# Two-part fp16 tables and states for the S5 scan of the first mixer, with the scan's inputs moved ahead in VectorE's order

## The chip, the cores and the metric

The kernel runs on one core of a Trainium2 chip. The metric is the device time of one execution in microseconds (us), as the median of several runs; less is better. The engines are named as in the profile: PE is TensorE's matrix products and PEld its weight loads, DVE is VectorE, ACT is ScalarE, POOL is GpSimd, and SP is SyncE, which here issues most of the transfers.

## The reference

The whole program is two residual networks one behind the other, at D = 1024 and T = 512 positions. Only the first mixer of the first one is touched. Its heart is S5: 32 groups of 16 channels, each with 64 complex states that decay and turn from position to position.

```
def _even_mixer(h, ...):
    proj = h @ w_in                       # 1024 -> 2048
    u_pool, u_ssm, z = proj[:512], proj[512:1024], proj[1024:]
    y_pool = _multiscale_pool(u_pool, pool_w, pool_scale)
    y_ssm = _s5(u_ssm, ...)
    return (concat(y_pool, y_ssm) * silu(z)) @ w_out

def _s5(u, log_dt, a, b, c, d_skip, w_glu):     # a, b, c complex
    abar = exp(a * dt); bb = (abar - 1) / a * b
    x[t] = abar * x[t-1] + bb @ u[t]            # 32 groups, 64 states
    y = real(c @ x) + d_skip * u
    val, gate = split(y @ w_glu)
    return val * sigmoid(gate)
```

## The kernel before, in words

**The projections.** Every large product is made in fp16 with both operands cut into a high and a low half: `form1` (L329 to 339) runs, for each of eight blocks of 128 rows, high by high (L336), low input by high weights (L337) and high input by low weights (L338), 24 products of 128x512 into one PSUM bank. `wload` and `wsplit` fetch a block of weights through SP's queue, write the high half on ACT (L283, with the factor `WS`) and the low half on DVE (L284). `split` (L290 to 292) does the same for activations, with the low half on POOL or on a given engine.

**The mixer.** `even` (L799 on) makes 16 projections of `ev_in` (384 products), then eight of `glu` (96) and eight of `ev_out` (192): 672 products in all. The first four are the scan's inputs: for each, DVE multiplies the PSUM bank by the norm's factor into `uS` (L821) and a DMA writes it to a buffer `ud` in device memory, from which it is read back in another layout. `s5_params` (L588 on) makes powers of the decay (`pr`, `pi`, by products at L563 to 568), the factors `k`, and the tables `bb` and `bd`.

**The scan** goes in four quarters q of eight groups each, in fp32. `s5_phases`, for each second quarter, makes tables of cosine and sine (`tr`, `ti`) by doubling, on DVE and POOL in turns, with the scratch tiles `ph`. `s5_tables` makes the output tables `CR` and `CI` on DVE with POOL's products `cw` (L702 to 708), the response of eight positions by products into `aq` (L714), which goes by `kt` and a buffer `kd` into eight shifted copies in `Tm` (SP's queue, L724), and the input tables: `bs` on DVE with `cw` on POOL (L733 to 735), turned on PE (L739) and copied by ACT to `bt` (L740). `s5_scan` loads `Ug`, runs 16 products of `bt` (L761), turns the result by four DVE products `sz` (L766 to 769), scans on DVE (L775, L776), turns back to the states `Sr` (DVE) and `Si` (POOL), and runs eight groups of three products into two banks: `Tm` by `Ug` (L787), `CR` by `Sr` (L788), `CI` by `Si` (L789). ACT copies them to `yg` (L791), which goes to device memory and back as `ys`.

**Behind the scan** in the code stand the four pool groups: a projection to the tile `up` (one buffer), running sums on POOL in `usa` and `usb` (one buffer each, L843), the difference `pd` on DVE (L846 to 848), another projection `zsp` and one fp32 product with `pool_w` (L854). Then come four gates `zs`, the `glu` products, which need `ys`, and `ev_out`.

**What sets the order.** The kernel is written on a tile scheduler, which puts each engine's instructions into one list, by the order of the code, a model of times, and the tiles that are free; on the chip each engine goes through its list in order. Projections take one of three PSUM banks `mm`; the first pool product and the norm use two banks `a`; the tables and the scan take turns on three banks `aq` by `aux()`. `mm()` looks at a list `self.first` first: its entries name the bank group of the next projections, before the standard `mm` holds. Ahead of the change the list is empty.

## Time and profile before

| | |
|---|---|
| median of 3 runs | 2562.06 us (2561.75 to 2565.82) |
| the profiled execution | 2564.81 us, span 2563.0 us |
| mean granted TensorE clock | 0.977 |
| PE busy | 2470.0 us (96%), 14547 instructions |
| PEld busy | 1255.7 us (49%) |
| DVE busy | 1363.2 us (53%) |
| ACT busy | 974.0 us (38%) |
| POOL busy | 738.9 us (29%) |
| DMA | 240.32 MB, 94 GB/s on average |

The span is the time from the first to the last instruction on the core; the execution's own time holds what lies around it, too. A matrix product's end is modelled and products are pipelined, so that one line of order of time says "0.38 us" for products that follow each other at 0.22. The granted clock is a share of TensorE's full speed. The first mixer fills the first 10% of the span.

### The profile page before, as it was taken

The numbers are of one execution on the slowest core, as the hardware profiler recorded it, in microseconds if no ns is written. First come the engines' busy times: TensorE is split into PE (matmuls) and PEld (weight loads), VectorE is DVE, ScalarE is ACT, GpSimd is POOL, SyncE is SP. The second block draws the span as 40 slices with busy tenths as digits, with TensorE's granted clock in tenths as the row PEclk, the third lists the DMA queues.
The fourth block names the chain that finished last, engine by engine and source line by source line (L and its number), as shares of the span: only waits on it lengthen the run. The fifth ranks groups of instructions, "written<-read, shape, count | busy, mean of one in ns | idle before, by whom it ended". The sixth has DMA issues, their size and how long they took to land.

```text
span 2563.0 us, 37095 instructions
## 1 busy us (share of the span) xinstructions
PE 2470.0 (96%) x14547; PEld 1255.7 (49%) x14547; DVE 1363.2 (53%) x2297; ACT 974.0 (38%) x1686; POOL 738.9 (29%) x634
## 2 busy tenths in 40 slices
PE   7998989999999999999999999999999999999998
PEld 3554434444444456674444444444457565444445
DVE  8846891753333577765433334333345777733334
ACT  4223666443322434333423223323223566523322
POOL 5611850333320244332333201333003121333300
PEclk9899989999999999999999999999999999999999
DMA  4223211233333432113333333333335101233333
GB/s 161 84 74 99 91 50 42 76 98 107 99 105 117 133 87 68 40 46 122 107 107 99 101 100 104 99 104 100 97 108 166 64 25 46 95 99 107 97 104 124
DMA packets 112440, 240.32 MB, mean 94 GB/s; under 512 B 39688, under 2 KB 51848, under 8 KB 112264
## 3 DMA queue, kind: packets, MB, share of 16 engines
q1 hardware_dynamic: 97760, 230.08, 29.3%
q10 hardware_dynamic: 14504, 7.87, 1.1%
q8 instruction: 114, 1.87, 0.3%
q14 instruction: 62, 0.51, 0.1%
HBM read 222.95 MB, written 7.34 MB: 90 GB/s over the span
## 4 chain that ended last, share of the span: by engine, by line
PE 83%; DVE 6%; issue 4%; POOL 3%; DMA 2%; ACT 2%; SPq 0%; ACTq 0%; POOLq 0%; DVEq 0%
PE b L337 17%; PE b L336 17%; PE b L338 17%; PE b L540 6%; PE b L541 6%; PE b L539 6%; POOL cv L966 2%; PE b L1205 1%; PE b L1626 1%; DVE wl L284 1%; PE mm L337 1%; PE mm L338 1%; PE mm L336 1%; PE b L1646 1%; PE b L1562 1%
## 5 line engine op out<-in xcount | busy, mean ns | idle before, releaser
L283 ACT ACTIVATE wh<-st 128x1024 f16<-128x1024 f32 (+6 forms) x432 | 422.7, 981 | 1069.0 <-PE b L337 666.9
L336 PE MATMUL b<-hh,wh 128*128 128x512 f16 x2096 | 799.0, 383 | 22.7 <-ACT hh L291 7.9
L337 PE MATMUL b<-hl,wh 128*128 128x512 f16 x2096 | 801.8, 383 | 1.2 <-POOL hl L292 1.0
L338 PE MATMUL b<-hh,wl 128*128 128x512 f16 x2096 | 799.8, 383 | 0.4 <-DVE wl L284 0.4
L284 DVE SCALAR_TENSOR_TENSOR wl<-st,wh 128x1024 f16<-128x1024 f32 (+6 forms) x432 | 507.3, 1176 | 367.5 <-ACT wh L283 365.9
L337 PEld LDWEIGHTS <-wh 128*128 128x128 f16 x2320 | 229.8, 99 | 300.8 <-issue 43.1
L336 PEld LDWEIGHTS <-wh 128*128 128x128 f16 x2320 | 230.2, 99 | 288.8 <-issue 24.3
L338 PEld LDWEIGHTS <-wl 128*128 128x128 f16 x2320 | 229.5, 99 | 284.8 <-issue 23.1
L539 PE MATMUL b<-fh,wh 128*128 128x512 f16 x660 | 250.1, 379 | 0.0
L540 PE MATMUL b<-fl,wh 128*128 128x512 f16 x660 | 250.1, 379 | 0.0
L541 PE MATMUL b<-fh,wl 128*128 128x512 f16 x660 | 250.1, 379 | 0.0
L528 POOL TENSOR_TENSOR sg<-sg,rho 128x512 f32<-128x512 f32 x88 | 153.6, 1747 | 292.6 <-ACT sg L527 282.0
L292 POOL TENSOR_TENSOR fl<-f,fh 128x512 f16<-128x512 f32 x88 | 139.9, 1590 | 265.6 <-ACT fh L291 265.4
L531 DVE SCALAR_TENSOR_TENSOR f<-b,sg 128x512 f32<-128x512 f32 x88 | 60.8, 691 | 246.0 <-PE b L338 239.9
L362 DVE TENSOR_TENSOR sg<-b,rho 128x512 f32<-128x512 f32 x88 | 60.4, 691 | 232.2 <-PE b L338 228.8
L292 POOL TENSOR_TENSOR hl<-nh,hh 128x512 f16<-128x512 f32 x42 | 54.6, 1307 | 288.3 <-ACT hh L291 288.3
L336 PE MATMUL mm<-hh,wh 128*128 128x512 f16 x224 | 88.3, 396 | 15.7 <-ACT hh L431 6.9
L539 PEld LDWEIGHTS <-wh 128*128 128x128 f16 x660 | 64.6, 98 | 78.0
L540 PEld LDWEIGHTS <-wh 128*128 128x128 f16 x660 | 64.6, 98 | 77.9
L541 PEld LDWEIGHTS <-wl 128*128 128x128 f16 x660 | 64.6, 98 | 77.8
L966 POOL TENSOR_TENSOR cv<-cv,cvt 128x512 f32<-128x512 f32 x60 | 88.0, 1469 | 14.5 <-ACT cvt L965 10.2
L337 PE MATMUL mm<-hl,wh 128*128 128x512 f16 x224 | 88.5, 397 | 3.0 <-DVE hl L432 2.2
(616 smaller groups left out, 3044.4 us busy)
## 6 DMA issues: line engine op xcount, KB each, us to landing
st<-in_gu_a SPq DMA_DIRECT2D x88, 512.0 KB, 3.5
st<-in_gu_b SPq DMA_DIRECT2D x88, 512.0 KB, 3.5
st<-in_dn_b SPq DMA_DIRECT2D x36, 512.0 KB, 3.5
st<-in_dn_a SPq DMA_DIRECT2D x32, 512.0 KB, 3.5
st<-in_od_in SPq DMA_DIRECT2D x24, 512.0 KB, 3.5
st<-in_ab_in SPq DMA_DIRECT2D x22, 512.0 KB, 3.5
st<-in_cd_in SPq DMA_DIRECT2D x16, 512.0 KB, 3.6
st<-in_ev_in SPq DMA_DIRECT2D x15, 512.0 KB, 3.7
```

The lines of the kernel that those rows point to most:

```text
L283: nc.scalar.activation(wh[:, s], st[:, s], AF.Copy, scale=WS)
L284: nc.vector.scalar_tensor_tensor(wl[:, s], st[:, s], WS, wh[:, s], op0=ALU.mult, op1=ALU.subtract)
L292: (eng or self.nc.gpsimd).tensor_sub(lo, src, hi)
L336: self.nc.tensor.matmul(ps, wh[:, s], xh[:, k], start=(k == 0), stop=False)
L337: self.nc.tensor.matmul(ps, wh[:, s], xl[:, k], start=False, stop=False)
L338: self.nc.tensor.matmul(ps, wl[:, s], xh[:, k], start=False, stop=(k == kn - 1))
L528: nc.gpsimd.tensor_mul(sg, sg, self.rho)
L531: nc.vector.scalar_tensor_tensor(f, ps, 1.0 / FS, sg, op0=ALU.mult, op1=ALU.mult)
L539: nc.tensor.matmul(ps, wh[:, s], fh[:, k], start=(k == 0), stop=False)
L540: nc.tensor.matmul(ps, wh[:, s], fl[:, k], start=False, stop=False)
L541: nc.tensor.matmul(ps, wl[:, s], fh[:, k], start=False, stop=(k == KF - 1))
L966: G.tensor_add(cv, cv, t)
```

## The change

Five numbers of the scan are put into fp16 halves, so that its products are made like the projections, in three passes (high by high, low by high, high by low) into the same banks.

- The inputs: behind each `uS`, ACT writes a high half and DVE a low half (`uh`, in the pool groups' tile `usa`), and `ud` and `Ug` hold two parts.
- `Tm`: the high half of `kt` on ACT, the low one on DVE, two parts of 128x1024 in fp16. Its 64 DMAs are shared: the high parts on SP's queue, the low ones on ACT's.
- The output tables: `s5c` is multiplied by `WS` once; `CR` and `CI` become scratch tiles (in the place of `bs0` and `bs1`), and a tile `C` takes their halves, the high ones by ACT, the low ones by POOL.
- `bt`: the high half on ACT with the factor `WS`, the low half on DVE straight from PSUM.
- The states: `Sp`, high by ACT, low by DVE.
- The factor's inverse `IWS` is taken in DVE's four products `sz` and in ACT's copies `yg`.

Two lines concern the order: `after()` gives the scheduler an edge without a semaphore, by which the first `CR` stands behind the last `uS` on DVE; and the first five projections take the banks `mm`, `mm`, `mm`, `aq`, `aq`.

```diff
+    def after(self, n, p):
+        self.tc.add_manual_dep(n.ins, p.ins.name, mybir.DependencyInfo(
+            mybir.DependencyClass.NoSync, mybir.DependencyReason.DATA), reason="in this order")
...
         nc.scalar.dma_start(S["c"], A["s5_c"])
+        nc.scalar.activation(S["c"], S["c"], AF.Copy, scale=WS)
...
-        CR = R["CR"] = qp.tile([P, 4, 9, 16], F32, name="CR")
-        CI = R["CI"] = qp.tile([P, 4, 9, 16], F32, name="CI")
+        CR = tp.tile([P, 4, 9, 16], F32, name="CR", tag="bs0")
+        CI = tp.tile([P, 4, 9, 16], F32, name="CI", tag="bs1")
...
-        V.tensor_tensor(CR, pw(pr), cb(0), op=ALU.mult)
+        n = V.tensor_tensor(CR, pw(pr), cb(0), op=ALU.mult)
+        if q == 0:
+            self.after(n, S["u"])
...
-        kt = tp.tile([P, P], F32, name="kt")
-        nc.scalar.activation(kt, ps, AF.Copy)
-        kd = self.dr.tile([P, P], F32, name=f"kd{q}")
+        kt = tp.tile([P, 2, P], F16, name="kt")
+        self.split(kt[:, 0], kt[:, 1], ps, V)
+        kd = self.dr.tile([P, 2, P], F16, name=f"kd{q}")
         nc.sync.dma_start(kd, kt)
-        Tm = R["T"] = qp.tile([P, 8, P], F32, name="Tm")
+        Tm = R["T"] = qp.tile([P, 2, 8, P], F16, name="Tm")
...
         for s in range(8):
-            nc.sync.dma_start(Tm[s * 16:(s + 1) * 16, :, (7 - s) * 16:P], kv[:, :, 0:(s + 1) * 16])
+            for e in range(2):
+                (nc.scalar if e else nc.sync).dma_start(
+                    Tm[s * 16:(s + 1) * 16, e, :, (7 - s) * 16:P], kv[:, e, :, 0:(s + 1) * 16])
+        C = R["C"] = qp.tile([P, 2, 2, 4, 8, 16], F16, name="C")
+        for r, t in enumerate((CR, CI)):
+            self.split(C[:, 0, r], C[:, 1, r], t[:, :, 1:9])
...
-            bt = qp.tile([P, 4, P], F32, name=f"bt{part}")
+            bt = qp.tile([P, 2, 4, P], F16, name=f"bt{part}")
...
-            nc.scalar.activation(bt, ps.rearrange("p (a b) -> p a b", a=4), AF.Copy)
+            nc.scalar.activation(bt[:, 0], ps, AF.Copy, scale=WS)
+            V.scalar_tensor_tensor(bt[:, 1], ps, WS, bt[:, 0], op0=ALU.mult, op1=ALU.subtract)
...
+        three = ((0, 0), (0, 1), (1, 0))
...
-                    nc.tensor.matmul(ps[hs, part, g], R["B"][part][:, g, hs], Ug[:, 2 * g + h], start=True, stop=True)
+                    for a, b in three:
+                        nc.tensor.matmul(ps[hs, part, g], R["B"][part][:, a, g, hs], Ug[:, b, 2 * g + h],
+                                         start=(a + b == 0), stop=(a == 1))
...
-        V.tensor_tensor(u[0], xr, ct, op=ALU.mult)
...
+        for o, x, y in zip(u, (xr, xi, xi, xr), (ct, st, ct, st)):
+            V.scalar_tensor_tensor(o, x, IWS, y, op0=ALU.mult, op1=ALU.mult)
...
+        Sp = qp.tile([P, 2, 2, 4, 64], F16, name="Sp", bufs=1)
+        for r, t in enumerate((Sr, Si)):
+            self.split(Sp[:, 0, r], Sp[:, 1, r], t, V)
...
-            nc.tensor.matmul(ps[:, g // 2], R["T"][:, g], Ug[:, g], start=True, stop=False)
-            nc.tensor.matmul(ps[:, g // 2], cr, Sr[h, g // 2], start=False, stop=False)
-            nc.tensor.matmul(ps[:, g // 2], ci, Si[h, g // 2], start=False, stop=True)
+            for a, b in three:
+                nc.tensor.matmul(ps[:, g // 2], R["T"][:, a, g], Ug[:, b, g], start=(a + b == 0), stop=False)
+            for r in range(2):
+                for a, b in three:
+                    c = R["C"][h, a, r, g // 2].rearrange("p j h -> p (j h)")
+                    nc.tensor.matmul(ps[:, g // 2], c, Sp[h, b, r, g // 2], start=False, stop=(r + a == 2))
...
+            self.first = ["mm", "mm", "mm", "aq", "aq"]
             uS = sp.tile([P, 4, 8, 64], F32, name="uS")
-            ud = self.dr.tile([4, 8, 16, 8, 64], F32, name="ud")
+            ud = self.dr.tile([4, 2, 8, 16, 8, 64], F16, name="ud")
...
-                V.tensor_mul(uS[:, m].rearrange("p s c -> p c s"), cs(ps), cs(self.rho))
-                nc.sync.dma_start(ud[m].rearrange("g h s c -> (g h) s c"), uS[:, m])
+                S["u"] = V.tensor_mul(uS[:, m].rearrange("p s c -> p c s"), cs(ps), cs(self.rho))
+                up = ek.tile([P, 2, 8, 64], F16, name="uh", tag="usa", bufs=1)
+                self.split(up[:, 0], up[:, 1], uS[:, m], V)
+                nc.sync.dma_start(ud[m].rearrange("e g h s c -> (g h) e s c"), up)
```

The lines of the changed kernel stand 5 or 6 further down in the first part and 13 to 23 further in the scan: the projection's products are L341 to 343, `uS` is L842, the input products L778, the output products of the states L809.

**On DVE, around the scan's inputs.** Before, the first three `uS` stand behind four table products, `CR` and `CI` (the names with `k` are small factors of the tables, `wl` a low half of weights):

```order
L655 TENSOR_TENSOR k_314<-k_314,k_315 128x16
L284 SCALAR_TENSOR_TENSOR wl<-st,wh 128x1024
L702 TENSOR_TENSOR CR<-pr,s5c 128x576 x2
L705 TENSOR_TENSOR CI<-pi,s5c 128x576 x2
L656 TENSOR_TENSOR ki<-k_314,den 128x16
L821 TENSOR_TENSOR uS<-mm,rho 128x64x8 x3
L704 TENSOR_TENSOR CR<-CR,cw_547 128x576
L708 SCALAR_TENSOR_TENSOR CI<-CI,cw_548 128x576
```

In the change the first two stand among the small products that make the powers (`pr`, `pw_0`), and the first low half `uh` follows:

```order
L656 TENSOR_TENSOR k_316<-pi,s5a 128x16
L644 TENSOR_TENSOR m_301<-m_301 128x16
L842 TENSOR_TENSOR uS<-mm,rho 128x64x8 x2
L636 TENSOR_TENSOR pr<-mag,cs 128x16
L645 TENSOR_TENSOR m_301<-m_301 128x16
L297 TENSOR_TENSOR uh<-uS,uh 128x512
L568 TENSOR_TENSOR pw_0_271<-pr 128x16
```

The inputs have moved ahead of the powers, and so of all tables.

**On PE, behind the outputs of the first scan.** Before, the last of its output products and the turning of a later `bs` are followed by projection products (`hh`, `wh`, `wl` are their halves):

```order
L787 MATMUL aq<-Ug,Tm 128x64
L788 MATMUL aq<-Sr,CR 128x64
L789 MATMUL aq<-Si,CI 128x64
L739 MATMUL aq<-ident,bs_730 128x128 x4
L338 LDWEIGHTS wl
L338 MATMUL mm<-hh,wl 128x512
L336 LDWEIGHTS wh
L336 MATMUL mm<-hh,wh 128x512
```

In the change the next scan's input products follow:

```order
L809 LDWEIGHTS C
L809 MATMUL aq<-Sp,C 128x64
L752 MATMUL aq<-ident,bs_871 128x128 x4
L778 LDWEIGHTS bt_863
L778 MATMUL aq<-Ug,bt_863 64x64
```

No projection product stands at this place any more.

**On PE, behind the outputs of the last scan.** Before, 314 projection products follow, the first of them in the midst of a group of 24:

```order
L787 MATMUL aq<-Ug,Tm 128x64
L788 MATMUL aq<-Sr,CR 128x64
L789 MATMUL aq<-Si,CI 128x64
L337 LDWEIGHTS wh
L337 MATMUL mm<-hl,wh 128x512
L338 LDWEIGHTS wl
L338 MATMUL mm<-hh,wl 128x512
```

In the change a pool product comes first, and then 432 projection products, with three more pool products among them:

```order
L809 LDWEIGHTS C
L809 MATMUL aq<-Sp,C 128x64
L877 MATMUL a<-pd,pool_w 128x512
L341 LDWEIGHTS wh
L341 MATMUL mm<-hh,wh 128x512
L342 LDWEIGHTS wh
L342 MATMUL mm<-hl,wh 128x512
```

So 118 projection products and all four pool products have moved behind the last scan.

## Rows read from the trace of the kernel before

**Rows 1.** Busy time by stretch: from:to, us, busy (instructions), PEclk, DMA share, GB/s.

```profile
24.00:72.00 48.00, 36.70 (x210) 17.86 (x209) 47.12 (x125) 13.71 (x19) 38.86 (x48) 0.83 0.32 99
110.00:120.00 10.00, 10.00 (x33) 7.05 (x33) 4.12 (x6) 1.59 (x4) 2.46 (x2) 0.51 0.42 122
165.00:238.00 73.00, 69.93 (x316) 31.00 (x315) 39.40 (x52) 28.49 (x46) 1.15 (x13) 0.98 0.38 117
```

**Rows 2.** PE in order of time: start us, us, instruction, [idle before <-releaser].

```profile
37.92 0.58 PE L336 MATMUL mm<-hh,wh 128*128 128x512 f16 x1 [6.44 <-DVE uS L821]
...
165.16 0.61 PE L337 MATMUL mm<-hl,wh 128*128 128x512 f16 x1
...
168.12 0.39 PE L338 MATMUL mm<-hh,wl 128*128 128x512 f16 x1
...
172.02 0.38 PE L338 MATMUL mm<-hh,wl 128*128 128x512 f16 x1
...
237.89 0.38 PE L338 MATMUL mm<-hh,wl 128*128 128x512 f16 x1
```

**Rows 3.** DVE in order of time, up to the first scan.

```profile
28.41 0.18 DVE L631 TENSOR_TENSOR pi<-mag,sn 128x16 f32<-128x16 f32 x1
...
31.80 0.18 DVE L655 TENSOR_TENSOR k<-k,k 128x16 f32<-128x16 f32 x1
...
36.85 2.79 DVE L821 TENSOR_TENSOR uS<-mm,rho 128x512 f32<-128x512 f32 x3
...
66.31 0.41 DVE L766 TENSOR_TENSOR sz<-aq,tr 128x252 f32<-128x252 f32 x1
```

**Rows 4.** PE in order of time, a pool product.

```profile
88.13 1.02 PE L854 MATMUL a<-pd,pool_w 128*128 128x512 f32 x2
```

**Rows 5.** DVE in order of time, subtractions and additions of the input tables.

```profile
88.54 0.68 DVE L735 TENSOR_TENSOR bs<-bs,cw 128x512 f32<-128x512 f32 x1
...
120.07 3.15 DVE L735 TENSOR_TENSOR bs<-bs,cw 128x512 f32<-128x512 f32 x2 [0.33 <-POOL cw L734]
```

**Rows 6.** Groups by line, DVE, 0 to 205 us: count | busy, mean ns | idle before.

```profile
L284 DVE SCALAR_TENSOR_TENSOR wl<-st,wh 128x1024 f16<-128x1024 f32 x18 | 24.0, 1341 | 2.6 <-ACT wh L283 2.6
```

**Rows 7.** POOL in order of time, its first large table product.

```profile
31.85 5.04 POOL L706 TENSOR_TENSOR cw<-pr,s5c 128x576 f32<-128x576 f32 x1 [1.10 <-DVE pr L567]
```

**Rows 8.** Groups by line, POOL, 24 to 160 us, shapes apart.

```profile
L734 POOL TENSOR_TENSOR cw<-pi,bb 128x512 f32<-128x512 f32 x8 | 10.9, 1368 | 5.1 <-DVE CR L704 4.4 <-DVE CI L708 0.7
L706 POOL TENSOR_TENSOR cw<-pr,s5c 128x576 f32<-128x576 f32 x4 | 9.1, 2280 | 1.1 <-DVE pr L567 1.1
...
L703 POOL TENSOR_TENSOR cw<-pi,s5c 128x576 f32<-128x576 f32 x4 | 5.9, 1483 | 0.0
L292 POOL TENSOR_TENSOR hl<-zsp,hh 128x512 f16<-128x512 f32 x4 | 5.5, 1364 | 11.8 <-ACT hh L291 11.8
```

**Rows 9.** Tile ph alone, by stretch: us, DVE and POOL busy, PEclk, DMA.

```profile
24.00:160.00 136.00, 21.61 (x42) 22.03 (x42) 0.87 0.29 86
```

**Rows 10.** The last scan in order of time, on DVE and POOL.

```profile
148.13 0.41 DVE L766 TENSOR_TENSOR sz<-aq,tr 128x252 f32<-128x252 f32 x1
...
154.00 0.80 POOL L568 TENSOR_TENSOR Si<-sz,sz 128x256 f32<-128x256 f32 x1
```

**Rows 11.** Groups by line, ACT, 0 to 205 us: copies out of PSUM.

```profile
L740 ACT ACTIVATE bt<-aq 128x512 f32<-128x512 f32 x8 | 4.7, 595 | 4.2 <-PE aq L739 4.2
L791 ACT ACTIVATE yg<-aq 128x256 f32<-128x256 f32 x4 | 1.5, 385 | 26.4 <-PE aq L789 26.4
```

**Rows 12.** PE in order of time, output products of the first scan.

```profile
78.46 0.43 PE L787 MATMUL aq<-Ug,Tm 128*128 128x64 f32 x2
...
79.41 0.43 PE L787 MATMUL aq<-Ug,Tm 128*128 128x64 f32 x2
```

**Rows 13.** PE in order of time, fp16 products of 64 columns in a later stage.

```profile
2008.88 0.29 PE L1656 MATMUL b<-nv,nat 128*128 128x64 f16 x4
```

**Rows 14.** Tile Tm, 0 to 200 us: durations ns min/median/max, first and last start.

```profile
L724 SPq DMA_DIRECT2D Tm<-kd x32: 318/428/752, 56.8 to 134.9; - x32
```

More of the change, by code (lines that the diff above doesn't have):

```diff
@@ L715, in s5_tables @@
             nc.tensor.matmul(o, S["bd"][:, 1, gg], CI[:, g, 0:8].rearrange("p j h -> p (j h)"), start=False, stop=True)
-        kt = tp.tile([P, P], F32, name="kt")
-        nc.scalar.activation(kt, ps, AF.Copy)
-        kd = self.dr.tile([P, P], F32, name=f"kd{q}")
+        kt = tp.tile([P, 2, P], F16, name="kt")
+        self.split(kt[:, 0], kt[:, 1], ps, V)
+        kd = self.dr.tile([P, 2, P], F16, name=f"kd{q}")
         nc.sync.dma_start(kd, kt)
-        Tm = R["T"] = qp.tile([P, 8, P], F32, name="Tm")
-        G.memset(Tm, 0.0)
-        kv = kd.rearrange("(g h) x -> h g x", h=16)
+        Tm = R["T"] = qp.tile([P, 2, 8, P], F16, name="Tm")
+        G.memset(Tm.bitcast(F32), 0.0)
+        kv = kd.rearrange("(g h) e x -> h e g x", h=16)
         for s in range(8):
-            nc.sync.dma_start(Tm[s * 16:(s + 1) * 16, :, (7 - s) * 16:P], kv[:, :, 0:(s + 1) * 16])
+            for e in range(2):
[4 more added lines that the diff above has]
+            self.split(C[:, 0, r], C[:, 1, r], t[:, :, 1:9])
         sh = [P, 4, 8, 16]
@@ L739, in s5_tables @@
                 nc.tensor.transpose(ps[:, i * P:(i + 1) * P], bs[:, i].rearrange("p s h -> p (s h)"), self.ident)
-            nc.scalar.activation(bt, ps.rearrange("p (a b) -> p a b", a=4), AF.Copy)
+            ps = ps.rearrange("p (a b) -> p a b", a=4)
+            nc.scalar.activation(bt[:, 0], ps, AF.Copy, scale=WS)
+            V.scalar_tensor_tensor(bt[:, 1], ps, WS, bt[:, 0], op0=ALU.mult, op1=ALU.subtract)
             R["B"].append(bt)
@@ L746, in s5_scan @@
         V, G = nc.vector, nc.gpsimd
-        Ug = qp.tile([P, 8, 64], F32, name="Ug")
-        uv = ud[q].rearrange("g h s c -> h s g c")
+        Ug = qp.tile([P, 2, 8, 64], F16, name="Ug")
+        uv = ud[q].rearrange("e g h s c -> h s e g c")
         for s in range(8):
             nc.sync.dma_start(Ug[s * 16:(s + 1) * 16], uv[:, 7 - s])
+        three = ((0, 0), (0, 1), (1, 0))
         br = qp.tile([P, 4, 64], F32, name="br")
@@ L765, in s5_scan @@
         u = [i[:, :, 0:63] for i in t]
-        V.tensor_tensor(u[0], xr, ct, op=ALU.mult)
-        V.tensor_tensor(u[1], xi, st, op=ALU.mult)
-        V.tensor_tensor(u[2], xi, ct, op=ALU.mult)
-        V.tensor_tensor(u[3], xr, st, op=ALU.mult)
+        for o, x, y in zip(u, (xr, xi, xi, xr), (ct, st, ct, st)):
+            V.scalar_tensor_tensor(o, x, IWS, y, op0=ALU.mult, op1=ALU.mult)
         V.tensor_add(br[:, :, 1:64], u[0], u[1])
@@ L784, in s5_scan @@
             h = slice((g % 2) * 64, (g % 2) * 64 + 64)
-            cr = R["CR"][h, g // 2, 1:9].rearrange("p j h -> p (j h)")
-            ci = R["CI"][h, g // 2, 1:9].rearrange("p j h -> p (j h)")
-            nc.tensor.matmul(ps[:, g // 2], R["T"][:, g], Ug[:, g], start=True, stop=False)
-            nc.tensor.matmul(ps[:, g // 2], cr, Sr[h, g // 2], start=False, stop=False)
-            nc.tensor.matmul(ps[:, g // 2], ci, Si[h, g // 2], start=False, stop=True)
+            for a, b in three:
[4 more added lines that the diff above has]
+                    nc.tensor.matmul(ps[:, g // 2], c, Sp[h, b, r, g // 2], start=False, stop=(r + a == 2))
         yg = ek.tile([P, 8, 64], F32, name="yg", bufs=1)
-        nc.scalar.activation(yg[:, 0::2], pe[:, 0:4], AF.Copy)
-        nc.scalar.activation(yg[:, 1::2], po[:, 0:4], AF.Copy)
+        nc.scalar.activation(yg[:, 0::2], pe[:, 0:4], AF.Copy, scale=IWS)
+        nc.scalar.activation(yg[:, 1::2], po[:, 0:4], AF.Copy, scale=IWS)
         nc.sync.dma_start(yd[q].rearrange("t h g c -> (t h) g c"), yg)
```

## The prediction

> **What bounds the kernel now.** I read the stretches of the first mixer first, then TensorE's and VectorE's order of time in them, then the costs of their instructions. TensorE (PE) is busy in 96% of the whole span, so what counts is when it gets through its list. The mixer's last projection product starts at 237.89 us, the last scan's outputs are finished at 165.16, and between them stand 314 products of 128x512 with little idle time [rows 1, 2]. Ahead of that PE is not full: it is busy for 36.70 of the 48 us from 24 to 72 [rows 1], 6.44 of them lost at 37.92 to the scan inputs uS, which VectorE (DVE) makes only at 36.85 [rows 2, 3]. DVE itself is busy for 47.12 of those 48 us and GpSimd (POOL) for 38.86 [rows 1]. So at first the tables are made by a full DVE and POOL while PE fills the time with projection products; after 165 us PE alone decides.
>
> **What the order changes.** It decides more than the number formats. Now 248 projection products (672 in the mixer, less 110 ahead of the first table products and 314 behind the last scan) lie between the products of the four scans and hide the scans' waits. In the new order 158 stand ahead of the first table products, 82 more up to the last scan's outputs, and 432 behind these, with the four pool products (L854) among them. Once scan 0 has begun, PE holds a single projection (24 products) up to the last scan's outputs. The cause is in the bank list: the fifth call of mm() takes an aq bank, which is given out after the 24 of the scans, and with it the first pool group, its single tile up and all that follows wait for scan 3. The comparison is therefore one of ends: when must the last scan's outputs be finished for 432 products to end where 314 end now?
>
> **Break-even.** A projection product takes 0.2167 us (18 of them from 168.12 to 172.02, [rows 2]); 432 take 93.6. Four pool products take 1.02 each [rows 4], 4.1. The first seven run slowly, as from 165.16 to 168.12 now: 2.96 us in place of 1.52, 1.4 more [rows 2]. Idle time stays: 165 to 238 holds 3.07 us of it now [rows 1]; the wait for the scan's output ys is part of that and will be covered by 88 products, so I take 2. Sum 101.1; the end now is 237.89 + 0.22 = 238.1. Hence the last scan must be through at **137.0 us**; each microsecond later is one lost, each earlier one gained. The stages after the mixer keep their work; the scheduler moved some rows in them, which I set at 0, with 3 either way for the range.
>
> **Up to the first scan.** Today the uS instructions stand behind four table products on DVE; now two of them stand just behind the instruction that starts at 28.41 [rows 3], so they begin at about 28.5 instead of 36.85 and PE's 6.44 us go. Then DVE has three uS (2.79), two low halves uh (0.68 each, as any such instruction of 512 elements, [rows 5]), a weight split (1.3, [rows 6]) and the small instructions that take it from 28.41 to 31.80 now [rows 3], some 8.4 us with their overlaps: 36.9. There POOL begins its tables, which is where it gets to work now too, its first being held up to 36.89 [rows 7]. So the early inputs free PE but not POOL. Up to what scan 0 needs, POOL has four cw of 128x576 (5.7: two L703, and two L706 without the one of 5.04 us), four cw of 128x512 (5.5), three new low halves of C (4.1, by the subtraction of the same shape) [rows 7, 8], and both phase tables: 22.0 us with the bb products [rows 9], of which the last two instructions, 0.8 each, are not needed. 35.7 us, so 72.6. A table step and a weight split on DVE and the hand-overs between the engines add 3.4 (at least 1, at most 7). Scan 0's first DVE instruction: **76 us**, against 66.31 now [rows 3].
>
> **A round, from one scan's first DVE instruction to the next one's.** (1) From there to the state Si DVE and POOL take 6.7 us in the last scan, a ys among it (148.13 to 154.80, [rows 10]). (2) Ahead of the state on DVE stand the next quarter's four bs: 0.68 each, 2.7; where POOL works two take 3.15, so 4.5 or more at worst [rows 5]. (3) The halves of the states are new: ACT's high and DVE's low half, 0.4 each (the yg copies are of 256 elements too, [rows 11]): 0.8. (4) 72 products in fp16. Now eight groups of three fp32 products take 0.95 us each [rows 12]; fp16 products of 64 columns with new weights follow each other at 0.03 us (four end 0.29 after the first starts, each being 0.19, [rows 13]): 2.2 for a scan. That is a real saving of 5.4 us of PE per scan, but it now lies in a chain in which PE waits. [...] I take the half rate: 4.3. (5) Two yg and two bt high halves on ACT [rows 11], one low half on DVE: 0.8 + 1.2 + 0.7 = 2.7. (6) Half of the Tm transfers are now issued from ACT's queue, and wait there for kd; three stand between yg and bt at 0.43 each [rows 14]: between 0 and 1.3, I take 0.6. (7) The second 24 of the scan's 48 input products: 0.7, or 1.4 at the half rate. Sum 6.7 + 2.7 + 0.8 + 4.3 + 2.7 + 0.6 + 1.4 = **19.2** (15.8 to 21.7). CR and CI of the next quarter lie in DVE's gap while PE and ACT are at work, and cost nothing as long as (4) to (7) last longer than their 2.7. The doubled Tm pieces and the Ug loads have a round's time and lie beside the chain. The scale factors ride in instructions that exist; the one on s5c is a short ACT instruction long before its use.
>
> **Sum.** 76 + 3 x 19.2 + 11.8 (the last round's 1, 3 and 4) = 145.4, that is 8.4 later than 137.0. The profiled execution took 2564.8, so 2573.2; it lies 2.7 above the median of the runs, 2562.1, so **2570.5**. With the lower bounds of the round it is 76 + 47.4 + 9.7 = 133.1 (4 faster), with the upper ones and 80 for the first scan 156.9 (20 slower). A measurement of this kernel tells some 0.2% from no change, 5.1 us.
>
> **Rivals.** (a) *PE keeps its full rate* in the short bursts: the round is 16.4, the last scan through at 134.9, the time 2560.0, no change to be told. Against it the 0.51 [rows 1]; for it, that fp16 passes are shorter and denser. (b) **Faster:** the chain hides behind DVE's own work, since POOL loses ten pool additions in this stretch and weight splits fall away. Then a round is what DVE itself has to do: 6.0 up to Sr, bs 2.7, CR and CI 2.7, bt 1.4, Sp 0.8, kt 0.3, 13.9 us [rows 5, 10]; 76 + 41.7 + 9.7 = 127.4, 9.6 faster, 2552.5. It decides where the round falls below 17. For it: nothing else stands in PE's queue, where scans are now held up by projections. (c) *DVE and POOL exclude each other.* A bs that takes 0.68 took 1.6 in the pair at 120.07 beside POOL [rows 5]. If each such instruction waits out the other engine's, a round is POOL's 11.7 (two cw of each kind and two C halves 8.3, four of the scan's 3.4 by Si's 0.80 and more, [rows 8, 10]) plus DVE's 9 on two SBUF inputs and 1.9 others, 22.6: 76 + 67.8 + 11.8 = 155.6, 2580.7. [...] (d) *ys holds DVE up.* It stands in DVE's queue ahead of the states; a wait for its transfer may return each round. I keep that within the upper bound.
>
> **Chances.** Forecast 0.45, (a) 0.22, (b) 0.18, (c) 0.15. Slower by over 0.2%: 0.35 of the forecast and all of (c), 0.50. Within it: the rest of the forecast, 0.10, of (a) 0.17, of (b) 0.01, together 0.28. Faster: 0.17 of (b) and 0.05 of (a), 0.22. The range runs from (b) to (c), 2552 to 2582; on the slower side alone it would be 2567 to 2582.
>
> **What would show it.** After: uS from about 28.5 and no wait of PE for it; scan 0 at 74 to 80; DVE idle for several microseconds a round, waiting for ACT's bt and yg; rounds of 18 to 21 us; a granted clock near 0.5 from 80 to 145; 432 products without gaps behind the last scan. Wrong if rounds are near 14 to 16, if PE holds its full rate there, or if the last outputs come ahead of 137 us.

## The result, and the profile after

The changed kernel takes **2592.99 us** (median; 2591.52 to 2601.98), the one before 2562.24 beside it: ratio 1.0124, 95% interval [1.0099, 1.0149], 31 us slower. The forecast was slower, but by 8.4 us, with 20 as the end of the range.

The profiled execution is the slowest of the four, 2601.98 us with a span of 2600.2, 37.2 above the one of before. Of these, 26.7 lie in the first mixer, whose last product moved from 237.89 [rows 2] to 264.57. Of the rest, 2.9 and 6.5 lie in two later stages (867 to 1232 and 1918 to 2224 us in the kernel before). All 17 kernels profiled here do the same work there, but the scheduler put it into another order in many of them, and these two stages took 358 to 372 and 303 to 312 us, without regard to which mixer was faster. Four other stages, whose order is the same in all 17, took 346.7, 343.3, 342.8 and 318.3 us in every one. In the second of the two the change's order took 311.2 to 312.0 in three kernels, the order of before 305.4 and 306.3 in two. So an edit can cost some 6 us in a stage that it does not touch, by the order there.

The change's own execution is late besides: its first `uS` starts at 31.77, and at 29.4 to 30.3 in the other fp16 versions. Without these 1.8 us (e3 and e5, with the same order up to there, start at 29.9), an estimate gives the mixer some 25 of the median's 31 and the later stages some 6.

The kernel before alone ran between 2557.85 and 2571.39 in 22 runs. So the mixer's end is compared in what follows beside the time, and of the times no difference under some 4 us is read.

Busy time by stretch in the kernel after, columns as in [rows 1]:

```profile
24.00:72.00 48.00, 42.78 (x206) 19.07 (x204) 44.24 (x127) 18.25 (x26) 29.21 (x50) 0.94 0.43 125
80.00:140.00 60.00, 24.34 (x315) 17.51 (x316) 45.45 (x68) 9.11 (x21) 31.86 (x34) 0.50 0.25 58
110.00:120.00 10.00, 3.44 (x38) 2.50 (x38) 9.26 (x12) 0.83 (x2) 5.75 (x8) 0.50 0.13 21
```

Up to 72 us PE has gained, as forecast (42.78 busy in place of 36.70). From 80 to 140 it is busy for 24.34 of 60 us, at a granted clock of 0.50. VectorE (DVE) in order of time, from the inputs to the last scan:

```profile
31.77 1.94 DVE L842 TENSOR_TENSOR uS<-mm,rho 128x512 f32<-128x512 f32 x2
...
70.80 0.86 DVE L708 TENSOR_TENSOR CR<-pr,s5c 128x576 f32<-128x576 f32 x1
71.59 0.87 DVE L713 TENSOR_TENSOR CI<-pi,s5c 128x576 f32<-128x576 f32 x1
...
77.37 1.27 DVE L755 SCALAR_TENSOR_TENSOR bt<-aq,bt 128x512 f16<-128x512 f32 x2
...
79.99 2.17 DVE L284 SCALAR_TENSOR_TENSOR wl<-st,wh 128x1024 f16<-128x1024 f32 x1
82.08 0.41 DVE L785 SCALAR_TENSOR_TENSOR sz<-aq,tr 128x252 f32<-128x252 f32 x1
...
90.20 1.43 DVE L568 TENSOR_TENSOR sz<-zr,tr 128x256 f32<-128x256 f32 x1
91.56 1.44 DVE L570 TENSOR_TENSOR sz<-zr,ti 128x256 f32<-128x256 f32 x1
...
105.27 0.42 DVE L785 SCALAR_TENSOR_TENSOR sz<-aq,tr 128x252 f32<-128x252 f32 x1 [0.28 <-PE aq L778]
...
115.05 1.43 DVE L297 TENSOR_TENSOR Sp<-Si,Sp 128x256 f16<-128x256 f32 x1
116.40 1.43 DVE L297 TENSOR_TENSOR Sp<-Sr,Sp 128x256 f16<-128x256 f32 x1
...
127.91 0.42 DVE L785 SCALAR_TENSOR_TENSOR sz<-aq,tr 128x252 f32<-128x252 f32 x1 [1.40 <-PE aq L778]
...
132.28 0.75 DVE L892 SCALAR_TENSOR_TENSOR ys<-uS,ev_vec,ys 128x512 f32<-128x512 f32 x1 [2.65 <-DMA Ug<-ud]
...
139.11 0.41 DVE L297 TENSOR_TENSOR Sp<-Si,Sp 128x256 f16<-128x256 f32 x1
...
149.31 0.42 DVE L785 SCALAR_TENSOR_TENSOR sz<-aq,tr 128x252 f32<-128x252 f32 x1 [1.40 <-PE aq L778]
...
153.73 0.75 DVE L892 SCALAR_TENSOR_TENSOR ys<-uS,ev_vec,ys 128x512 f32<-128x512 f32 x1 [2.69 <-DMA ys<-yd]
```

The scans begin at 82.08, 105.27, 127.91 and 149.31, so the rounds are 23.2, 22.6 and 21.4. PE in order of time: the output products of scan 1, the last of scan 3, the mixer's end.

```profile
117.89 0.48 PE L809 MATMUL aq<-Sp,C 64*128 64x64 f16 x10 [2.13 <-DVE Sp L297]
...
122.11 0.50 PE L809 MATMUL aq<-Sp,C 64*128 64x64 f16 x6
...
162.10 0.50 PE L809 MATMUL aq<-Sp,C 64*128 64x64 f16 x6
...
264.57 0.38 PE L343 MATMUL mm<-hh,wl 128*128 128x512 f16 x1
```

The last scan is through at 162.6, in place of the 145.4 forecast and the 137.0 needed; behind it lie 102.0 us to the last product's start at 264.57, where the sum had 100.9 (101.1 to its end). So the comparison of ends held, and the 17.2 us by which the forecast missed the last output lie ahead of 162.6.

### The profile page after: what moved, and what is told of

Same layout as the page of the kernel before. It is cut to its first block, busy times and chain, and to the rows that moved or that the text cites. A ratio compares the mean times of both kernels' runs of the same rounds, so it can differ in the third digit from the quotient of the medians.

```text
span 2600.2 us, 37533 instructions
## 1 busy us (share of the span) xinstructions
PE 2467.7 (95%) x14707; PEld 1252.3 (48%) x14707; DVE 1377.3 (53%) x2321; ACT 982.8 (38%) x1707; POOL 742.3 (29%) x642
## 4 chain that ended last, share of the span: by engine, by line
PE 81%; DVE 6%; issue 4%; POOL 3%; ACT 2%; DMA 2%; SPq 1%; POOLq 0%; DVEq 0%; ACTq 0%
PE b L341 16%; PE b L342 16%; PE b L343 16%; PE b L546 5%; PE b L545 5%; PE b L544 5%; POOL cv L989 2%; PE b L1228 1%; PE b L1649 1%; PE mm L342 1%; PE mm L341 1%; PE mm L343 1%; DVE wl L284 1%; PE b L1669 1%; PE b L1585 1%
## 5 line engine op out<-in xcount | busy, mean ns | idle before, releaser
L341 PE MATMUL b<-hh,wh 128*128 128x512 f16 x2096 | 797.3, 382 | 26.7 <-ACT hh L296 9.4
L341 PEld LDWEIGHTS <-wh 128*128 128x128 f16 x2320 | 229.8, 99 | 292.7 <-issue 24.4
L989 POOL TENSOR_TENSOR cv<-cv,cvt 128x512 f32<-128x512 f32 x60 | 88.5, 1478 | 14.5 <-ACT cvt L988 10.2
L341 PE MATMUL mm<-hh,wh 128*128 128x512 f16 x208 | 81.2, 394 | 10.9 <-ACT hh L436 8.1
L342 PE MATMUL mm<-hl,wh 128*128 128x512 f16 x208 | 81.3, 393 | 3.3 <-DVE hl L437 3.2
```

The costliest lines, as they stand in the source:

```text
L341: self.nc.tensor.matmul(ps, wh[:, s], xh[:, k], start=(k == 0), stop=False)
L342: self.nc.tensor.matmul(ps, wh[:, s], xl[:, k], start=False, stop=False)
L989: G.tensor_add(cv, cv, t)
```

## The experiments

Each kernel was timed beside the kernel before (medians of 2562.96 to 2564.61). Times in us; all but the median are from one profiled execution of each kernel. `sz` is a scan's first DVE product, so a round runs from one scan's first `sz` to the next one's. The gap is the idle time of PE behind the last output, up to the mixer's last product:

| | first sz | rounds, last part | last output | mixer's last product | gap | median |
|---|---|---|---|---|---|---|
| before | 66.3 | 28.4, 28.6, 24.8, 17.1 | 165.2 | 237.9 | 3.1 | 2562.2 |
| the change | 82.1 | 23.2, 22.6, 21.4, 13.3 | 162.6 | 264.6 | 2.2 | 2593.0 |
| e1 list of 4 | 83.3 | 37.4, 24.6, 18.9, 14.2 | 178.5 | 246.5 | 9.1 | 2571.7 |
| e2 fp32, list of 5 | 68.3 | 26.7, 22.3, 21.6, 17.2 | 156.1 | 256.2 | 1.9 | 2583.7 |
| e3 ys late | 80.3 | 23.2, 22.0, 18.7, 12.7 | 156.8 | 258.2 | 2.6 | 2585.5 |
| e4 Tm on SP | 80.0 | 22.2, 28.3, 17.4, 15.5 | 163.4 | 270.3 | 5.7 | 2602.7 |
| e5 bt early | 76.1 | 23.5, 23.5, 20.3, 13.1 | 156.5 | 257.6 | 2.5 | 2590.1 |
| e6 no cw | 77.1 | 21.4, 20.0, 20.7, 13.7 | 152.8 | 253.9 | 1.9 | 2579.0 |
| e15 low halves on ACT | 74.1 | 20.6, 19.9, 18.5, 11.8 | 144.9 | 246.7 | 3.0 | 2575.3 |

**What takes the cover away: the bank list or the format?** The cover is the projection products that keep PE busy while the scans wait. Two kernels part the two causes. The first is the change with

```diff
-            self.first = ["mm", "mm", "mm", "aq", "aq"]
+            self.first = ["mm", "mm", "mm", "aq"]
```

> The changed kernel with the bank list shortened by its fifth entry, so that the first pool group's projection takes a standard bank again; all fp16 parts stay. PE then has projection products and pool products among the scans' products, and 261 projection products in place of 432 behind the last scan's outputs. Theory (the order, through the bank list, took the cover from PE): PE is busy nearly throughout from 80 to 160 us, its granted clock there is over 0.8, the rounds may take 20 to 27 us, the last outputs come at 160 to 175 us, and 261 products take 57 behind them: the mixer ends at 219 to 235 against 238 before, so 2540 to 2562 us, 30 to 50 below the change. Rival (the splits, their queueing and the sharing of DVE and POOL cost it, whatever PE has to do meanwhile): within 8 of the change, 2583 to 2603.

It took 2571.71, ratio to before 1.0036 [1.0025, 1.0048]: 21 us less than the change, from one entry of a list. 261 products now stand behind the last scan. Its stretch from 80 to 140 us:

```profile
80.00:140.00 60.00, 52.01 (x396) 25.41 (x394) 53.40 (x79) 17.06 (x32) 43.35 (x51) 0.94 0.28 75
```

PE is busy for 52.01 in place of 24.34, at 0.94. The theory holds for the cover; the time lies 10 above its range, since the last outputs came at 178.5 and not by 175, and PE then waited (below). The second is the kernel before, all in fp32, with the list of five and nothing else:

> The kernel before with the list of five banks alone, everything in fp32. PE has 432 projection products behind the last scan and one group of 24 among the scans, as in the change. Theory (the list is the cause): slower than before by 20 to 45, 2582 to 2607 us, with a granted clock near 0.5 among the scans. Rival (the fp16 parts are the cause): within 8 of before, 2554 to 2570.

It took 2583.73, 1.0079 [1.0061, 1.0098], 20 slower than before, and PE's row from 80 to 140 us shows a granted clock of 0.50 again (34 projection products still lie among its scans, where 24 were expected):

```profile
80.00:140.00 60.00, 48.57 (x283) 40.04 (x282) 31.07 (x46) 6.44 (x14) 20.19 (x24) 0.50 0.21 57
```

So the list costs some 20 us in either format (18.1 and 18.3 at the mixer's end), and the fp16 parts with the cover another 8 to 9; the rival that the format alone is the cause falls.

The change without its edge of `after()` was not run. But the early inputs need neither the edge nor the list nor the halves `uh`: e8 below has the states' products in fp16 and nothing else, and its DVE begins the inputs as early, ahead of the first large table product:

```profile
29.37 1.93 DVE L829 TENSOR_TENSOR uS<-mm,rho 128x512 f32<-128x512 f32 x2
...
36.26 1.75 DVE L706 TENSOR_TENSOR CI<-pi,s5c 128x576 f32<-128x576 f32 x1
```

With the list alone, in e2, they start at 37.96, behind four table products as before. So the output tables' new form brings the inputs forward; which part of it does so (the scaled `s5c`, or `CR` and `CI` as scratch tiles) is not shown.

**What makes the exposed rounds long?** Five kernels with the list of five, as in the change. First, the early ys instructions behind the last scan's states:

```diff
-                V.scalar_tensor_tensor(v, uS[:, m]..., vec[:, 1, m:m + 1], v, ...)
+                n = V.scalar_tensor_tensor(v, uS[:, m]..., vec[:, 1, m:m + 1], v, ...)
+                self.after(n, self.last)      # the last low half of Sp
```

> The changed kernel with the three early ys instructions placed behind the last scan's states on DVE. In the change's trace DVE waits 2.65 and 2.69 us for ys in two rounds, with 0.75 for the instruction itself, ahead of the scan instruction zr. Theory (these waits lie in the chain): 5 to 7 us less than the change, 2586 to 2588. Rival (zr waits just as long for POOL's bi or another transfer): within 2 of the change, 2591 to 2595.

2585.50, 7.5 less. The third round fell from 21.4 to 18.7, the last part from 13.3 to 12.7, the others by 0.6 at most, 3.9 in all. The waits for ys lie in the chain: `zr` stands right behind them. The mixer ends 6.3 earlier, but 1.8 of that lie ahead of the first scan, where this kernel is the changed one: so much differs between executions. In the later stages e3 has nearly the order of the kernel before, and part of the 7.5 lies there.

The transfers of `Tm` all on SP:

```diff
-                (nc.scalar if e else nc.sync).dma_start(
+                nc.sync.dma_start(
```

> The changed kernel with all 64 Tm transfers issued from SP. In the change's trace three of them stand on ACT between yg and bt in two rounds and take 1.27 with 0.94 of idle time behind. Theory (they lengthen the round): 3 to 6 us less, 2587 to 2590. Rival (SP's queue then holds up the transfers of yg, ys and kd behind the Tm ones): no gain, or slower by up to 6, 2592 to 2599.

2602.65, 10 more: the rival holds, though the loss is above its range. The second round became 28.3 long, and PE's order of time names the transfer that came too late there:

```profile
128.95 1.50 PE L778 MATMUL aq<-Ug,bt 128*64 128x64 f16 x48 [8.36 <-DMA Ug<-ud]
```

The scan's inputs `Ug` stand in SP's queue, from 126.17 on, behind transfers of `Tm` (from 111.48) and ys (from 122.03). In the last part PE waited another 5.76 for `Tm` itself. The first scan came 2.1 earlier and the other two rounds were shorter, so the last output came only 0.8 later than in the change. Another 5 us were lost behind it, 3.6 of them in gaps, and the rest of the 10 after the mixer. The change's sharing of the queues is the better one, though ACT pays for it: its order of time in the change has

```profile
65.05 4.00 ACTq L733 DMA_DIRECT2D Tm<-kd  x8
69.10 1.09 ACT L754 ACTIVATE bt<-aq 128x512 f16<-128x512 f32 x2 [10.50 <-DMA Tm<-kd]
...
122.65 1.27 ACTq L733 DMA_DIRECT2D Tm<-kd  x3
123.97 1.09 ACT L754 ACTIVATE bt<-aq 128x512 f16<-128x512 f32 x2 [0.94 <-issue]
```

Next, DVE's order ahead of the first scan. In the rows above, ACT's high halves `bt` are through at 70.2, but DVE's low ones start only at 77.37, behind `CR`, `CI`, `tr` and `ph` for later quarters:

```diff
-        if q == 0:
-            self.after(n, S["u"])
+        self.after(n, S["u"] if q == 0 else self.btl)   # the last low half of bt
...
+            if e and not j:                             # second pair's phase tables
+                for i in k:
+                    self.after(i, self.szl)             # the first scan's last sz
```

> The changed kernel with edges for DVE's order: the next quarter's first CR product stands behind this quarter's low halves of bt, and the second pair's phase tables behind the first scan's products sz. In the change's trace the first bt low half starts at 77.37, 7.2 us behind ACT's high half, with the next quarter's CR and CI and four ph products ahead of it on DVE. Theory (DVE's order holds the first scan up): the first sz at 72 to 75 instead of 80 to 83, and 3 to 8 us less in all, 2585 to 2590. Rival (what was moved comes back inside the first two rounds): first sz early, but the last outputs and the time within 2 of the change, 2591 to 2595.

2590.08, 2.9 less, at the edge between theory and rival; the mixer ended 7.0 earlier. The low halves moved to 67.98, but the first `sz` only to 76.06 (DVE's rows):

```profile
67.98 1.28 DVE L758 SCALAR_TENSOR_TENSOR bt<-aq,bt 128x512 f16<-128x512 f32 x2
...
76.06 0.41 DVE L788 SCALAR_TENSOR_TENSOR sz<-aq,tr 128x252 f32<-128x252 f32 x1
```

In between PE was still at the 25 projection products that stand ahead of the scan's in its list, and the tables that were put off fill DVE in the first round. So DVE's list and PE's were two waits side by side, each hiding much of the other.

POOL's share: `cw` left out in the three later quarters, DVE reading a broadcast input instead.

```diff
-        G.tensor_tensor(w[0], pw(pi), cb(1), op=ALU.mult)
+        if not q:
+            G.tensor_tensor(w[0], pw(pi), cb(1), op=ALU.mult)      # and so for the other three
```

> The changed kernel without POOL's table products cw in the three later quarters: DVE takes a broadcast input in their place, so the tables of these quarters leave out the cross terms. DVE keeps its instructions, POOL loses 12 of 0.8 to 2.7 us. In the change's trace DVE's instructions last 5.4, 4.9, 1.8 and 1.4 us longer in the three rounds and the last part than the shortest of the same shape. Theory (DVE and POOL hold each other up): that excess falls under 2 a round, the rounds from 22.4 to 18 to 20 us, the time to 2580 to 2587. Rival (a round is set by hand-overs between DVE, ACT and PE, the products on POOL lie beside them): rounds within 1 us, 2589 to 2595.

2578.98, 14 less (1.0054 [1.0034, 1.0075] to before), and 10.7 less at the mixer's end; the rounds fell by 1.8, 2.7 and 0.7, and the first `sz` came 3 to 5 earlier. What DVE's instructions last longer than the shortest of their shape fell from 5.4, 4.9 and 1.8 us to 2.7, 2.2 and 1.7. The theory holds in part: some 5 us in the rounds, and 3 to 5 ahead of them, where POOL was free earlier. Groups by line, DVE, first in the change from 80 to 160 us, then without `cw` from 77 to 140:

```profile
L297 DVE TENSOR_TENSOR Sp<-Si,Sp 128x256 f16<-128x256 f32 x4 | 2.7, 670 | 0.1
```

```profile
L297 DVE TENSOR_TENSOR Sp<-Si,Sp 128x256 f16<-128x256 f32 x3 | 1.2, 414 | 0.0
```

Last, the low halves themselves. ACT writes a copy of the high half in their place:

```diff
-            V.scalar_tensor_tensor(bt[:, 1], ps, WS, bt[:, 0], op0=ALU.mult, op1=ALU.subtract)
+            nc.scalar.activation(bt[:, 1], ps, AF.Copy, scale=WS)      # kt, Sp and uh likewise
```

> The changed kernel itself with the low halves of uh, kt, bt and Sp written by ACT as copies of the high ones; the correction terms are left out. Here DVE waits 4 to 7 us in each round. Theory (in each round two low halves of bt and two of Sp lie in the chain, and the first bt one is held up behind tables): first sz at 72 to 76 instead of 80 to 83, rounds 1 to 2 us shorter, 2575 to 2585. Rival (ACT, with its Tm transfers, takes over the delay): 2588 to 2595.

2575.27, 17.7 less, at the better end of the theory's range. The first `sz` comes at 74.06, the rounds are 2.6, 2.7 and 3.0 shorter, the last outputs end at 144.9, and the mixer's last product is that of PE's row

```profile
246.67 0.38 PE L343 MATMUL mm<-hh,wl 128*128 128x512 f16 x1
```

101.8 behind the last output, as in the change. So in a chain without cover, 24 instructions that lasted 15 us in all in the change cost 18.

**With cover: what remains, and is there a version that beats before?** In e1 PE has less to do than in the kernel before, and still ends 8.6 later. Its order of time behind the last output:

```profile
178.12 0.34 PE L809 MATMUL aq<-Sp,C 64*128 64x64 f16 x6
...
187.56 1.44 PE L341 MATMUL mm<-hh,wh 128*128 128x512 f16 x3 [9.10 <-ACT hh L296]
```

It has run out of work and waits 9.1 us for `ys` and its halves: now the scan chain sets the end. Eight kernels shorten it or fill PE otherwise. With the edges of e3 and e5 and a third kind, in the list of four:

```diff
             R["B"].append(bt)
+        for t in tms:               # ACT's transfers of Tm
+            self.after(t, n)        # the last high half of bt
```

> The kernel of the first experiment (four entries in the list) with three edges for the order: late ys, bt low halves ahead of the next quarter's tables, and ACT's Tm transfers behind the bt high halves. 288 projection products stand behind the last scan. Theory (with cover on PE, what is left of the loss is the scan chain's queueing, 8 at the first scan and 3 a round): last outputs at 160 to 168 instead of 178, 2552 to 2564, no slower than before. Rival (DVE is full up to 145 us, and its work comes back wherever it is put): 2567 to 2573.

2574.55, 1.0042 [1.0026, 1.0057]: by the time the rival, and 1.6 above its range. The first `sz` came at 77.0 and the last output at 174.5, 4 earlier than in e1, but the rounds of 32.9 and 33.0 gave most of it back. The mixer ended at 241.7, 4.8 earlier than in e1; the later stages, in the change's order, ate that up. With the states' products alone in fp16 (`C` and `Sp`; low halves on DVE):

```diff
-            nc.tensor.matmul(ps[:, g // 2], cr, Sr[h, g // 2], start=False, stop=False)
-            nc.tensor.matmul(ps[:, g // 2], ci, Si[h, g // 2], start=False, stop=True)
+            for r in range(2):
+                for a, b in ((0, 0), (0, 1), (1, 0)):
+                    c = R["C"][h, a, r, g // 2].rearrange("p j h -> p (j h)")
+                    nc.tensor.matmul(ps[:, g // 2], c, Sp[h, b, r, g // 2], start=False, stop=(r + a == 2))
```

> The kernel before with the states' products alone in two fp16 parts (C and Sp; low halves on DVE), and inputs, Tm and bt in fp32 as before; no bank list, no edge. PE saves 16 fp32 products of about 0.3 us in each scan for 48 shorter ones, some 10 us of its list; DVE gains 1.4 for the halves of C and 0.8 for those of Sp in each quarter. Theory (half of the PE gain can be had without a longer way to the first scan): 2550 to 2560, faster than before. Rival (DVE, full up to 100 us, passes its 2.2 a quarter on): 2562 to 2572.

2571.73, 1.0033 [1.0021, 1.0044], at the rival's upper end: first `sz` at 75.0, last output at 177.0, 261 products behind it and 9.0 of gap, nearly e1's picture with half the change. Then the gates' loop was written ahead of the pool groups', so that gates fill PE first:

```diff
+            zs = []
+            for i in range(4):
+                ps = self.form1(A["ev_in"][12 + i], KD, hh, hl)
...
             for g in range(4):
                 ps = self.form1(A["ev_in"][4 + g], KD, hh, hl)
```

> The kernel of the first experiment (four entries in the list) with the four gates zs written ahead of the pool groups, so that their 96 projection products are the first to fill PE among the scans; a gate asks one multiplication of DVE, a pool group two, with the difference pd, and running sums of 1.4 to 2 us each of POOL. In that experiment's trace DVE is busy for 45.7 of the 48 us from 72 to 120 and POOL for 39.6. Theory (the pool groups' share of DVE and POOL is what keeps the covered fp16 version behind): rounds shorter by 3 to 6 in the first two, 2555 to 2567. Rival (the pool groups only move from one round to the next): 2568 to 2575.

2579.24 [1.0034, 1.0067], 7.5 more than e1: neither; the last output came at 179.8, with a second round of 34.5.

The same loop in the kernel before:

> The kernel before with the gates zs ahead of the pool groups, nothing else. Its first two rounds take 28 us. Theory (as for the version in fp16): 2 to 4 less a round, last outputs at 155 to 162, 339 products behind them, 2553 to 2562. Rival (PE is full from 72 us on either way): within 3 of before, 2560 to 2566.

2559.38 (2555.25 to 2567.51), ratio 0.9984 [0.9971, 0.9997]: some 4 us less than before, the only kernel of the study whose interval lies below it. The last output came at 159.2, 6 earlier, with 339 products behind it, as the theory has it. But the mixer's last product came at 238.4 and not ahead of 237.9, so the gain is not the mixer's: it lies in the two later stages.

> The gates first with the three edges of the seventh experiment (late ys, bt low halves early, ACT's Tm transfers behind bt), four entries in the list. 288 products behind the last scan. If both theories hold, they add: last outputs at 158 to 168, 2548 to 2562. If DVE's work only moves: 2568 to 2576.

This is e7 with e9's loop. 2573.68 [1.0022, 1.0048]: last output at 171.4, and no gain in time over e1. Yet the mixer ended at 237.5, as early as before: all that this version loses, it loses in the later stages, which took 371.6 and 309.7 us (364.9 and 305.4 before).

> The kernel of the eighth experiment (the states' products alone in fp16) with the gates first. 261 products behind the last scan, which came at 177.0 and left PE 9 us idle for ys. Theory: last outputs at 165 to 172, 2556 to 2566. Rival: 2568 to 2574.

This is e8 with e9's loop. 2564.27, 0.9992 [0.9983, 1.0002]: no different from before, and inside the theory's range. But the last output came at 177.7 and the mixer's last product at 244.9, 7 later than before, so it too gains in the later stages, and the theory's way there is not shown. Last, e1 with e15's copies by ACT, without and with those of `C`:

```diff
-            self.split(C[:, 0, r], C[:, 1, r], t[:, :, 1:9])
+            for i in range(2):
+                nc.scalar.activation(C[:, i, r], t[:, :, 1:9], AF.Copy)
```

> The kernel of the first experiment (four entries in the list) with the low halves of uh, kt, bt and Sp written by ACT as a second copy of the high half, so that DVE loses its 24 instructions for them (some 13 us in all); the products' low passes run on copies, so the correction terms are left out. Theory (the low halves on DVE, which is full from 72 to 120 us, keep the covered fp16 version 8 us behind the kernel before): last outputs at 163 to 170 instead of 178, 2557 to 2565. Rival (the price is elsewhere: POOL's halves of C, hand-overs, or the order of what fills PE): 2568 to 2575.

> As the thirteenth, with the low halves of C written by ACT as copies too, so that POOL loses its eight instructions for them (1.4 each): the correction terms of C are left out as well. If POOL's sharing with DVE is a further part: 3 to 6 less than the thirteenth. If DVE's own list is all: within 2 of it.

2573.57 [1.0026, 1.0058] and 2572.13 [1.0025, 1.0054]: no gain in time over e1. With cover, DVE's low halves are not what is left in the mixer (e13 ends it at 247.3, e1 at 246.5), though without cover they cost 18. With those of `C` off POOL too, the last output came at 171.3 instead of 180.2 and the mixer's last product at 238.5, as early as before, but the time does not show it.

It does not, because of the two later stages. Kernels that have the same order in both of them took (us; the last column is the median's loss to before, less the loss at the mixer's end):

| same order in both | first stage | second stage | lost outside the mixer |
|---|---|---|---|
| before, e13 | 364.9, 365.4 | 305.4, 306.3 | 0, 0.1 |
| the change, e5, e7 | 367.7, 365.5, 368.0 | 312.0, 311.2, 311.9 | 4.1, 7.4, 7.8 |
| e6, e10, e12 | 360.9, 364.5, 357.8 | 307.1, 303.1, 306.9 | 0.0, -5.8, -7.4 |

So the covered fp16 versions have two losses. One is in the mixer, 8.6 us in e1 and none in e11 and e14, whose chains are through at 171; no version ends the mixer clearly ahead of before. The other lies in the later stages and goes with their order, which no edit here aimed at. What in these orders costs the time is **open**, and so is what the other covered versions lose in the mixer: their first scans start 8 to 18 us later than before, and the order of what fills PE changes with every edit.

## Why the prediction was right in direction and wrong in size

**Right: the cause.** The bank list takes 118 products and the pool groups out from among the scans; e1 and e2 show it in both formats, 21 and 20 us. The comparison of ends was right to 1 us. In e15 the last output came at 144.9, close to the forecast's 145.4, and the mixer ended at 246.9, close to 238.1 + 8.4. For the part behind the last output that is a test; for the part ahead of it, it is chance, since e15 leaves out low halves that the forecast had counted.

**Right: early inputs.** The first two `uS` start at 31.77 (29.4 to 30.3 in the other fp16 versions; forecast 28.5), and no wait of PE for them is left.

**Wrong: 76 us for the first scan** (82.1; 80.3 in e3, alike up to there). The term that failed is the 3.4 for "a table step and a weight split on DVE and the hand-overs": the low halves of `bt` stand in DVE's list behind 6.6 us of tables for later quarters (70.80 to 77.37), and behind them stand 3.5 us more, a table step and the weight split `wl`, ahead of `sz`. I had priced the hand-over, not the place in the list. e5 and e15, which take the low halves from there, start the first scan at 76.1 and 74.1, so the place is worth 4 to 6 us. It is the whole list ahead of `sz` that counts. In e4, which has no Tm issues on ACT, the low halves come 4.5 earlier than in the change and the first `sz` only 2.1, since tables and the split now stand between the two (DVE's rows of e4):

```profile
72.86 1.27 DVE L755 SCALAR_TENSOR_TENSOR bt<-aq,bt 128x512 f16<-128x512 f32 x2
...
79.97 0.41 DVE L785 SCALAR_TENSOR_TENSOR sz<-aq,tr 128x252 f32<-128x252 f32 x1
```

So ACT's eight Tm issues, 4.00 us ahead of the high halves in the change, were not it.

**Wrong: the round of 19.2**, which was 22.4 on average and makes 9.6 of the 17.2 (the first scan 6.1, the last part 1.5). By its steps, in the second round: from the first `sz` to Si 7.0 (forecast 6.7); from there to the states' last half 5.6 in place of 2.7 + 0.8; the 72 products 4.8 (4.3); copies, ACT's transfers and `bt` 3.9 (3.3); the rest of the input products 1.4 (1.4). The clock forecast, half rate, was right: 0.50 from 80 to 140 us. No run shows the 4.3 itself, for which I had chosen the half rate between two values; in its place the trace shows 4.8 for the 72 products (and 1.4 for the second half of the input products). What failed are steps (1) to (3), the way from the first `sz` to the states' last half, with durations of an undisturbed DVE and no wait in its list: forecast 10.2, it took 13.8, 12.6 and 12.0 in the three rounds, and the rest 9.4, 10.1 and 9.5 in place of 9.0. What made it longer changes from round to round. In the first it was two products `sz` of 1.43 and 1.44 (0.39 and 0.94 in the second) and a weight split of 1.21; in the second the states' low halves, 1.43 each (0.41 to 0.43 in all other rounds); in the third the wait for ys. The four long ones stand beside these POOL rows:

```profile
89.76 1.60 POOL L711 TENSOR_TENSOR cw<-pi,s5c 128x576 f32<-128x576 f32 x1 [1.41 <-DVE bs L748]
91.32 1.39 POOL L714 TENSOR_TENSOR cw<-pr,s5c 128x576 f32<-128x576 f32 x1
...
114.60 1.60 POOL L711 TENSOR_TENSOR cw<-pi,s5c 128x576 f32<-128x576 f32 x1 [2.32 <-DVE bs L748]
116.16 1.40 POOL L714 TENSOR_TENSOR cw<-pr,s5c 128x576 f32<-128x576 f32 x1
```

Each half ends some 0.3 behind the POOL instruction that it met (116.48 and 117.83, to 116.20 and 117.56), and so does each of the two `sz` in the first round. Without `cw` (e6) the first round's way to Si takes 9.8 instead of 11.8, and the second's from Si to the last half 3.0 instead of 5.6. The four `sz` that read PSUM, and `bt`, which does too, kept 0.41 and 0.68 throughout. That is rival (c), whose round of 22.6 was nearly met; for pairs like these the trace agrees with it, though by what means the one engine holds the other up no run shows. But (c) priced every instruction so, and not every one was hit: e6 gives some 5 us in the rounds for all that `cw` cost there, of the 9.6 missed.

**Wrong: (d) kept within a bound.** The ys waits, 2.65 and 2.69 with 0.75 each, were in the third round and the last part; e3 gives 3.9 for them in the chain, so (d) was a term, and not a mishap. Of the last part, 13.3 in place of 11.8, they explain 0.6.

**Wrong: the later stages at 0.** The forecast knew that the scheduler had moved rows there, and allowed 3 us. The median lost 31 where the mixer's end lost 26.7, and e5 and e7, whose order there is the change's, lose 7.4 and 7.8 outside the mixer: 4 to 8 us, a term in place of nothing.

The parts overlap: by the medians ys 7.5, `cw` 14, low halves 17.7 and the cover 21 sum to more than the 31 lost. Part of that is the later stages' order, which each of these edits changed. That in a chain without cover each edit also shortens waits of the others is likely, but no kernel here joins two of these edits.

## What to carry to other kernels

A format that makes products cheaper on the busiest engine need not pay: here PE's saving lay in stretches where PE waited, and the splits lay in the chain it waited for. Look first at what an order or a buffer list does to the work that fills the gaps; one entry was two thirds of the loss. When a chain loses its cover, cost its instructions at what they last beside the other engine (the states' low halves took 1.43 us beside POOL's `cw` and 0.41 without it), in list order, with every in-order wait ahead of them (2.65 and 2.69 us for ys). And before a few microseconds are put down to an edit, compare the instruction lists and lengths of the stages that it does not touch.

## What was not expected of the hardware

Stages whose instruction lists are the same in all 17 kernels took the same time to 0.1 us in four cases (346.7, 343.3, 342.8 and 318.3), whatever stood ahead of them. Two stages of the same work in different order varied by 14 and 9 us (358 to 372, 303 to 312), so that a mixer that ends 8 us earlier (e14 against e1) need not show in the median; kernels with one order still differ by up to 7 and 4 there. And moving 32 small transfers from ACT's queue to SP's, which was to spare ACT 1.3 us a round, cost 10 us, with waits of 8.36 and 5.76 in the scans for transfers on that queue.
